# A decoder block's MLP: the second stage by seven block products instead of eight, with its operand sums made in the first stage

## The chip, the cores and the metric

The kernel runs on one core of a Trainium2 chip. The metric is the device time of one execution in microseconds (us), lower is better. All tensors are float32. The kernel that is changed is called before, the other one after. Line numbers (L923) are those of the kernel whose profile or listing is spoken of.

## The reference, cut to what matters

```python
# x: (1, 2048, 1024); D_MODEL = 1024; D_FF = 4096; one layer
h = _rmsnorm(x, norm_pre_mix)
...                                   # projections, attention, gated MLP, merge, w_out
x = x + _rmsnorm(y, norm_post_mix)

h = _rmsnorm(x, norm_pre_mlp)                                # 2048 x 1024
a = relu(einsum('bsd,df->bsf', h, w_mlp_in))                 # MLP, first stage: 2048 x 4096
y = einsum('bsf,fd->bsd', a * a, w_mlp_out)                  # MLP, second stage: 2048 x 1024
x = x + _rmsnorm(y, norm_post_mlp)
```

The change concerns the last four lines: two matrix products of 2048 x 1024 x 4096 each, a squared ReLU between them and a norm with a residual sum behind them.

## The kernel before, in words

Every float32 product is made of three reduced ones. `split` (L68) writes an operand as a rounded upper part, by an ACT copy at L71 or a POOL one at L73, and the rest, by a subtraction at L76. `mm3` (L85) then issues upper x upper, upper x rest and rest x upper (L86 to L88), all summed in one PSUM bank. `split_in` (L78) loads with a DMA on the SP queue (L82) and splits. So one block product 128 x 128 by 128 x 512 costs three matmuls on PE (TensorE). The order of the matmuls is the order in which the code issues them; the other engines' instructions are put in order by a scheduler, and each engine, the SP queue among them, runs its list strictly in that order.

The tokens are cut into two halves of 1024 (`half`; half 1 first), and each half into two blocks of 512. Ahead of the MLP, `out_block` (L754 and on) writes for each 128 tokens the sum `x` to `x1_d`, the normalized and transposed `h` to `h2_d`, and five sums of blocks of `h` (called T1 to T4 and B22) to `t_d` (L822). The sums of one half are gathered in the tile `tail` ahead of the last of these stores.

**The MLP's first stage** (about 1500 to 2147 us) already uses the scheme of Strassen and Winograd: a 2 x 2 by 2 x 2 block product by seven block products instead of eight. A pair `q` of two tiles of 128 of the 4096 (f) channels, with the depth 1024 cut in two, is one operand (A11 to A22 and the sums S1 to S4); two blocks of 512 tokens, cut along the depth as well, are the other one (B11, B21, B22 and the sums T1 to T4). `product(half, q, i)` issues product `i` of 12 matmuls (L918), so that the stage has 16 pairs x 2 halves x 7 x 12 = 2688 matmuls. `load_a` fetches the raw weights of a pair, 1 MB, into one of three buffers (L887); `sum_a` makes S1 to S4 of them on POOL (L899 to L902) and splits them. `places` gives the order: products 1 and 2 need only A11, A12, B11 and B21, so that at the beginning of a half those of `LEAD` = 5 pairs run ahead of the first product that needs a T; at its end those of `TRAIL` = 3 pairs do. `load_t` loads and splits a T block. The seven products are added as they come: ACT takes product 1 out of PSUM (`xs`), DVE adds products 6 and 7 to it (`u6`, `u7`, L937), and the four results are formed by L941 on DVE. ACT then applies the ReLU (L942; L933 for the first result), POOL squares (L922), and L923 stores the result with 2 KB rows to `s_d[f]`, four stores of 256 KB for a pair.

**The MLP's second stage** (2147.4 to 2846.0 us) is a plain product. It handles one half at a time, and in it groups of four f tiles. `load_w2` and `load_s` fetch and split a group's weights and squares one group ahead. `mlp_out` runs over eight blocks of 128 tokens and two width halves of 512 and issues 4 x 3 matmuls for each (L86 to L88); DVE copies (L1137) or adds (L1139) the bank to the running sum `acc`, of which there is one of 128 x 1024 for each of the eight token blocks. In a half's last group each block is ended at once: ACT squares with a row sum (L1142), POOL multiplies by the gain (L1143), DVE adds two row sums (L1145) and takes a root with ACT's help (`rstd_of`, L93 to L99), then multiplies and adds the residual from `x1_d` (L1150), and SP stores the result. The stage has 2 halves x 8 blocks x 2 x 32 tiles x 3 = 3072 matmuls.

## Time and profile before

| | |
|---|---|
| time, median of 3 runs | 2857.97 us (2854.01 to 2858.14) |
| time of the profiled execution | 2858.39 us |
| its span, from the first to the last record | 2856.3 us |
| granted TensorE clock, mean over the span | 0.989 |
| PE busy | 2787.4 us, 98% of the span, 13748 matmul records |
| DVE, ACT, POOL busy | 1464.7, 861.0, 760.5 us |
| DMA moved | 442.88 MB, mean 155 GB/s |

The profile is of one execution. An engine's busy time is the union of its instructions, without waits. A group row gives busy time and mean nanoseconds of one instruction, then the idle time ahead of them and what ended it, after an arrow. A window row gives its length, then for PE, PEld (weight loads, which overlap PE), DVE, ACT and POOL the busy time with the number of instructions, then the granted clock (1.00 is full), the DMA engines' busy share and GB/s. A row of a transfer group gives the number of transfers, KB of each and the median us from issue to landing. A row of the timeline gives the start, the length, the engine, and in square brackets the wait ahead and its releaser.

### The profile page before, as it was taken

The page shows a single profiled execution, that of the slowest core. Times are in us where ns is not written, and L with a number is a line of the kernel's source. Part 1 is how long each engine was busy: PE and PEld are TensorE (multiplying, and loading weights), DVE is VectorE, ACT ScalarE, POOL GpSimd, SP SyncE. Part 2 cuts the span into 40 slices and gives each one's busy share as a digit, 9 for nine tenths or more (in the row PEclk, how much of TensorE's full clock was granted, in tenths as well). Part 3 has the DMA queues.
Part 4 walks back from the last instruction along what each step waited for, and adds up shares of the span by engine and source line. Part 5 has one row for each costly group of instructions (what it writes and reads, how often), then busy time and mean ns, then how long its engine had stood idle before and what let it go on. Part 6 is the DMA issues. An engine that isn't in the chain of part 4 may idle for free.

```text
span 2856.3 us, 36699 instructions
## 1 busy us (share of the span) xinstructions
PE 2787.4 (98%) x13748; PEld 2347.7 (82%) x13748; DVE 1464.7 (51%) x2557; ACT 861.0 (30%) x1799; POOL 760.5 (27%) x591
## 2 busy tenths in 40 slices
PE   8999999999999999999998999999999999999998
PEld 8889888988878888777776888788878888888887
DVE  5654562434443353656556644654457444665445
ACT  5213111244443321443444433443332111211111
POOL 0340341200000023213026654555531001321012
PEclk9999999999999999999998999999999999999999
DMA  7544445465666563656467334633335223452232
GB/s 258 176 149 154 164 144 172 145 206 178 200 206 200 162 202 126 199 168 183 143 186 256 133 104 147 203 129 115 121 123 178 92 96 96 147 168 91 89 96 96
DMA packets 248849, 442.88 MB, mean 155 GB/s; under 512 B 18144, under 2 KB 106464, under 8 KB 248672
## 3 DMA queue, kind: packets, MB, share of 16 engines
q1 hardware_dynamic: 248672, 440.55, 47.8%
q8 instruction: 108, 1.77, 0.3%
q14 instruction: 69, 0.57, 0.1%
HBM read 299.77 MB, written 140.71 MB: 154 GB/s over the span
## 4 chain that ended last, share of the span: by engine, by line
PE 80%; DMA 6%; DVE 4%; POOL 4%; issue 4%; ACT 2%; SPq 0%; DVEq 0%; POOLq 0%; ACTq 0%
PE y L87 8%; PE y L86 8%; PE y L88 8%; PE ab L918 7%; PE ac L918 5%; PE aa L918 4%; PE g L88 4%; PE g L86 4%; PE g L87 4%; PE x L86 3%; PE x L87 3%; PE x L88 3%; PE pv L597 2%; DMA g<-gated 1%; PE pT L578 1%
## 5 line engine op out<-in xcount | busy, mean ns | idle before, releaser
L87 PE MATMUL y<-w,s 128*128 128x512 f32 x1024 | 399.6, 390 | 0.0
L86 PE MATMUL y<-w,s 128*128 128x512 f32 x1024 | 399.2, 390 | 0.0
L88 PE MATMUL y<-w,s 128*128 128x512 f32 x1024 | 398.3, 389 | 0.0
L71 ACT ACTIVATE s<-s 128x512 fp32r<-128x512 f32 x128 | 80.7, 632 | 494.1 <-DMA s<-sd 451.9
L1139 DVE TENSOR_TENSOR acc<-acc,y 128x512 f32<-128x512 f32 x240 | 159.2, 682 | 130.8 <-PE y L88 130.8
L86 PEld LDWEIGHTS y<-w,s 128*128 128x128 f32 x1024 | 192.2, 188 | 41.2
L88 PEld LDWEIGHTS y<-w,s 128*128 128x128 f32 x1024 | 192.2, 188 | 40.7
L87 PEld LDWEIGHTS y<-w,s 128*128 128x128 f32 x1024 | 192.3, 188 | 39.8
L73 POOL TENSOR_SCALAR w<-w2r 128x1024 fp32r<-128x1024 f32 x64 | 68.8, 1075 | 514.2 <-DVE acc L1139 253.8
L922 POOL TENSOR_TENSOR c<-c 128x512 f32<-128x512 f32 x128 | 151.4, 1184 | 201.4 <-ACT c L942 158.8
L918 PE MATMUL aa<-B,A 128*128 128x512 f32 x768 | 191.6, 402 | 8.4 <-ACT A L71 5.5
L918 PE MATMUL ab<-T,S 128*128 128x512 f32 x768 | 188.7, 394 | 9.8 <-ACT T L71 6.3
L918 PEld LDWEIGHTS aa<-B,A 128*128 128x128 f32 x768 | 147.6, 193 | 44.9 <-ACT A L71 6.8
L918 PEld LDWEIGHTS ab<-T,S 128*128 128x128 f32 x768 | 145.4, 190 | 42.9 <-ACT T L71 7.5
L86 PE MATMUL x<-hT_a,wq 128*128 128x512 f32 x384 | 149.7, 390 | 0.0
L88 PE MATMUL x<-hT_a,wq 128*128 128x512 f32 x384 | 149.4, 389 | 0.0
L87 PE MATMUL x<-hT_a,wq 128*128 128x512 f32 x384 | 149.4, 389 | 0.0
L73 POOL TENSOR_SCALAR w_g<-w_g_r 128x1024 fp32r<-128x1024 f32 x32 | 34.4, 1075 | 412.3 <-PE g L88 358.6
L76 DVE TENSOR_TENSOR w<-w2r,w 128x1024 fp32r<-128x1024 f32 x64 | 79.1, 1236 | 109.8 <-POOL w L73 109.8
L76 DVE TENSOR_TENSOR s<-s 128x512 fp32r<-128x512 f32 x128 | 93.5, 739 | 68.8 <-ACT s L71 68.1
L604 DVE TENSOR_REDUCE o<-po 128x256 f32<-128x512 f32 x48 | 33.2, 691 | 183.8 <-PE po L603 183.8
L71 ACT ACTIVATE S<-w1r 128x512 fp32r<-128x512 f32 x96 | 60.2, 631 | 154.9 <-PE ab L918 88.5
(276 smaller groups left out, 6546.5 us busy)
## 6 DMA issues: line engine op xcount, KB each, us to landing
sd<-c SPq DMA_DIRECT2D x128, 256.0 KB, 2.2
w1r<-in_w_mlp_in_dram SPq DMA_DIRECT2D x32, 1024.0 KB, 5.3
w2r<-in_w_mlp_out_dram SPq DMA_DIRECT2D x64, 512.0 KB, 3.6
s<-sd SPq DMA_DIRECT2D x128, 256.0 KB, 4.5
qk<-hl SPq DMA_DIRECT2D x24, 1024.0 KB, 5.3
qq<-qk SPq DMA_DIRECT2D x96, 256.0 KB, 5.0
w_g_r<-in_w_in_dram SPq DMA_DIRECT2D x32, 512.0 KB, 5.3
gated<-gt SPq DMA_DIRECT2D x64, 256.0 KB, 2.9
```

The costliest lines, as they stand in the source:

```text
L71: act.activation(hi, src, AF.Copy)
L73: pool.tensor_scalar(hi, src, 1.0, 1.0, op0=OP.mult, op1=OP.mult)
L76: (pool if lo_eng == "pool" else dve).tensor_sub(lo, src, f32(hi))
L86: pe.matmul(ps, lh, rh, start=start, stop=False)
L87: pe.matmul(ps, lh, rl, start=False, stop=False)
L88: pe.matmul(ps, ll, rh, start=False, stop=stop)
L578: pe.transpose(pt[:, off:off + P], e[:, b, hf * P:(hf + 1) * P], ident)
L597: pe.matmul(pv[:, o0:o0 + w_], l, r, start=n == 0, stop=n == len(mms) - 1, skip_group_check=True)
L604: dve.tensor_reduce(ot[:, :, j * 64:(j + 1) * 64], po.rearrange("p (b h e) -> p b e h", b=4, h=2), axis=AX.X, op=OP.add)
L918: pe.matmul(p, w[:, l, k, :], h[:, r, k, :], start=i in (1, 6, 5) and not k and not n, stop=k == 3 and n == 2, skip_group_check=True)
L922: pool.tensor_mul(t, t, t)
L1139: dve.tensor_add(an, an, p)
```

## The change: what it does

The second stage also becomes a 2 x 2 by 2 x 2 block scheme with seven products. Its blocks are: two blocks of 128 tokens, one from each 512-token block of a half (so a *token block* is one of eight pairs of these); two f tiles (a pair `q` of the first stage); two width halves of 512. One step (`ysteps`) is one group `g` of two pairs at one token block: seven products of 2 x 3 = 6 matmuls. There are 8 groups x 8 token blocks = 64 steps, and 64 x 42 = 2688 matmuls. The groups are the outer loop, so that the sums `acc` of all 2048 tokens stay on the chip (16 tiles of 4 KB per partition), and the weights are read once.

The operands of the left side, four squares and three sums, are made in the first stage: ACT now does ReLU and square (`square`), POOL makes four sums of squares for a pair (it did four squares), and `store_s` writes all seven to a new `s_d`, seven stores of 256 KB with 512-byte rows. The result tiles that are summed live longer, and SBUF is shared out anew: raw weights in five tiles of 512 KB instead of three of 1 MB, `c` tiles 3 instead of 6, `LEAD` 4 instead of 5. The T tiles of the first half are allocated up front in another order; `T2` no longer lies at the address of `tail`.

```diff
-    s_d = dtile([NF, P, S], "sd")
+    s_d = dtile([NF // 2, 2, P, 4, 7, P], "sd")
...
-    NQ, LEAD, TRAIL = NF // 2, 5, 3
+    NQ, LEAD, TRAIL = NF // 2, 4, 3
...
     def load_a(half, q):
-        raw = wp3.tile([P, 2, KT, P], F32, name=f"w1r_{half}{q}", tag="w1r", bufs=3)
-        sp.dma_start(raw.rearrange("p f k c -> p f (k c)"),
-                     a["w_mlp_in"][2 * q:2 * q + 2].rearrange("f p k c -> p f (k c)"))
-        araw[half, q] = raw
+        araw[half, q] = []
+        for f in range(2):
+            raw = wp3.tile([P, KT, P], F32, name=f"w1r_{half}{q}{f}", tag="w1r", bufs=5)
+            sp.dma_start(raw, a["w_mlp_in"][2 * q + f])
+            araw[half, q].append(raw)
...
-        def out_tile(f, ci, t):
-            pool.tensor_mul(t, t, t)
-            sp.dma_start(s_d[f, :, half * HALF + ci * 512:half * HALF + (ci + 1) * 512], t)
+        def store_s(o, t):
+            sp.dma_start(s_d[q, half][:, :, o, :], t.rearrange("p (i c) -> p i c", i=4))
+
+        def square(t, src):
+            act.activation(t, src, AF.Relu)
+            act.activation(t, t, AF.Square)
...
         elif i == 3:
-            output(0, 1, u_[half, q, 6], p)
+            a11, a12, a21, a22 = c1_[key], xs_[key], u_[half, q, 6], u_[half, q, 7]
+            output(a21, p)
+            s1, s2, s4 = (cp3.tile([P, 512], F32, name=f"s{n}_{nm}", tag="c", bufs=3) for n in (1, 2, 4))
+            pool.tensor_add(s1, a21, a22)
+            store_s(4, s1)
+            pool.tensor_sub(s2, s1, a11)
+            store_s(2, s2)
+            pool.tensor_sub(a21, a11, a21)
+            store_s(3, a21)
+            pool.tensor_sub(s4, a12, s2)
+            store_s(6, s4)
...
+    OPS = ("B11", "B21", "T2", "T3", "T1", "T4", "B22")
+    RIGHT, LEFT = 4, 14
+    def op_w2(q, name):
+        m = n_op[0] % (RIGHT + LEFT)
+        n_op[0] += 1
+        pl = r4 if m < RIGHT else bL
+        w = pl.tile([P, 2, 512], F32R, name=f"{name}y_{q}", tag="w2", bufs=RIGHT if m < RIGHT else LEFT)
+        raw = w2r_[q][:, dict(B11=0, B21=2, T2=4, T3=1, T1=0, T4=2, B22=3)[name]]
+        split(w[:, 0], w[:, 1], raw, "act", "pool")
+        w2_[q, name] = w
+    def load_s(n):
+        g, half, i = ysteps[n]
+        for q in (2 * g, 2 * g + 1):
+            pl = r4 if n % 3 == 0 else bL
+            w = pl.tile([P, 2, 7, P], F32R, name=f"s_{n}{q}", tag="s", bufs=2 if n % 3 == 0 else 4)
+            split_in(w, s_d[q, half][:, i], None, "act")
+            st_[n, q] = w
+    def yproduct(n, i):
...
+        which = {1: "a", 6: "a", 7: "a", 4: "a", 2: "b", 5: "c", 3: "c"}[i]
+        if i in (1, 2, 5):
+            ybank[n, which] = psum_any(f"y{which}_{n}")
...
+        if (half, b, ci, nh) in begun:
+            dve.tensor_add(an, an, p)
+        else:
+            begun.add((half, b, ci, nh))
+            dve.tensor_copy(an, p)
+        if g == NQ // 2 - 1:
+            left[n, ci] = left.get((n, ci), 4 if not ci else 3) - 1
+            if not left[n, ci]:
+                finish(half, b, ci)
+    yorder = sorted((7 * n + t, n, i) for n in range(len(ysteps))
+                    for i, t in ((1, 0), (2, 3), (6, 4), (7, 8), (5, 9), (4, 12), (3, 13)))
```

`yproduct` issues one product's six matmuls and then the DVE copy (L1207) or add (L1204) of its bank. `yorder` interleaves neighbouring steps: for PE the order is product 1 of step n, 7 and 5 of step n-1, 2 and 6 of step n, 4 and 3 of step n-1. Products 1, 6, 7 and 4 of a step use one bank after another, each adding on top. The loads of `s` go two steps ahead, into three sets of two buffers of 448 KB. `sum_w2` makes the sums of a pair's weights on POOL, and `op_w2` splits the seven operands with ACT and POOL during the group before. `finish` is the old end of a token block (squares, gain, root, residual), now for all sixteen blocks inside the last group's eight steps.

The following rows are the instructions in the order in which the built program has them, at three places. A row gives the line, the operation, output<-inputs and the shape; the digits behind a name tell its half and pair or its step.

The SP queue at the beginning of the MLP's first stage, before. `td_81` is the last store of T sums from `tail`, the `w1r` are raw weights by pair:

```order
L923 DMA sd_82<-c11_0_12938 128x512
L887 DMA w1r_10_13270<-in_w_mlp_in_dram 128x2x1024
L822 DMA td_81<-tail_12725 2560x1x128
L887 DMA w1r_11_13272<-in_w_mlp_in_dram 128x2x1024
L82 DMA T2_1_13263<-td_81 128x1024 x2
L82 DMA ar1_13_13310<-in_w_mlp_in_dram 128x512
L82 DMA T3_1_13329<-td_81 128x1024 x2
L887 DMA w1r_12_13336<-in_w_mlp_in_dram 128x2x1024
```

The same place after:

```order
L888 DMA w1r_100_13274<-in_w_mlp_in_dram 128x1024
L821 DMA td_81<-tail_12725 2560x1x128
L888 DMA w1r_101_13276<-in_w_mlp_in_dram 128x1024
L888 DMA w1r_110_13278<-in_w_mlp_in_dram 128x1024
L81 DMA T2_first_13267<-td_81 128x1024 x2
L888 DMA w1r_111_13280<-in_w_mlp_in_dram 128x1024
L888 DMA w1r_120_13282<-in_w_mlp_in_dram 128x1024
L888 DMA w1r_121_13284<-in_w_mlp_in_dram 128x1024
L81 DMA T3_first_13266<-td_81 128x1024 x2
```

The first pair's weights now come in two loads, the second of them behind the `td` store; three loads of 512 KB stand between `T2` and `T3`, and no lone `ar` load.

DVE at the start of the second stage, before. The c tiles are the last results of the first stage, `w2` and `s` are operands of the second one, `y` its banks:

```order
L941 TENSOR_TENSOR c11_015_17765<-u7_015_17750,ac_015_17752 128x512
L941 TENSOR_TENSOR c10_015_17782<-xs_015_17470,ab_015_17689 128x512
L941 TENSOR_TENSOR c01_015_17799<-u6_015_17702,ac_015_17752 128x512
L76 TENSOR_TENSOR w2_14_18013<-w2r_14_18014,w2_14_18013 128x1024
L1137 COPY acc10_17877<-y_1000_17885 128x512
L1137 COPY acc10_17877<-y_1001_17893 128x512
L1137 COPY acc11_17878<-y_1010_17901 128x512
L76 TENSOR_TENSOR s_120_17856<-s_120_17856 128x512
```

The same place after (`s_10` and `s_11` belong to step 1, `s_20` and `s_21` to step 2; `ya_0` is the first bank of step 0):

```order
L942 TENSOR_TENSOR u7_015_18023<-u7_015_18023,ac_015_18025 128x512
L942 TENSOR_TENSOR xs_015_17720<-xs_015_17720,ab_015_17954 128x512
L942 TENSOR_TENSOR u6_015_17967<-u6_015_17967,ac_015_18025 128x512
L75 TENSOR_TENSOR s_10_18162<-s_10_18162 128x896
L75 TENSOR_TENSOR s_11_18166<-s_11_18166 128x896
L75 TENSOR_TENSOR s_20_18174<-s_20_18174 128x896
L1207 COPY acc100_18189<-ya_0_18182 128x512
L1204 TENSOR_TENSOR acc100_18189<-acc100_18189,yb_0_18191 128x512
L75 TENSOR_TENSOR s_21_18178<-s_21_18178 128x896
L1207 COPY acc100_18189<-ya_0_18182 128x512
```

Three splits of `s` now stand ahead of the first copy, and a fourth between the second and the third reading of a bank.

DVE inside the second stage, before, where one group's adds and the next group's splits alternate:

```order
L1139 TENSOR_TENSOR acc16_17883<-acc16_17883,y_11260_18965 128x512
L1139 TENSOR_TENSOR acc16_17883<-acc16_17883,y_11261_18979 128x512
L1139 TENSOR_TENSOR acc17_17884<-acc17_17884,y_11270_18993 128x512
L76 TENSOR_TENSOR w2_120_19021<-w2r_120_19022,w2_120_19021 128x1024
L1139 TENSOR_TENSOR acc17_17884<-acc17_17884,y_11271_19007 128x512
L76 TENSOR_TENSOR s_1220_19052<-s_1220_19052 128x512
L76 TENSOR_TENSOR s_1221_19056<-s_1221_19056 128x512
L76 TENSOR_TENSOR s_1230_19065<-s_1230_19065 128x512
L1139 TENSOR_TENSOR acc10_17877<-acc10_17877,y_11600_19073 128x512
```

After, one step's worth of DVE (`ya_29` is the first bank of step 29, `yc_28` the third bank of step 28, `s_306` and `s_307` the operands of step 30):

```order
L1204 TENSOR_TENSOR acc010_18493<-acc010_18493,ya_29_20095 128x512
L1204 TENSOR_TENSOR acc001_18501<-acc001_18501,ya_28_20035 128x512
L75 TENSOR_TENSOR s_306_20027<-s_306_20027 128x896
L1204 TENSOR_TENSOR acc001_18501<-acc001_18501,yc_28_20110 128x512
L75 TENSOR_TENSOR s_307_20031<-s_307_20031 128x896
L1204 TENSOR_TENSOR acc010_18493<-acc010_18493,yb_29_20118 128x512
L1204 TENSOR_TENSOR acc010_18493<-acc010_18493,ya_29_20095 128x512
L1204 TENSOR_TENSOR acc001_18501<-acc001_18501,ya_28_20035 128x512
L1204 TENSOR_TENSOR acc000_18431<-acc000_18431,yc_28_20110 128x512
```

Two splits of 896 columns stand in every step between the adds, at fixed places of the cycle; the splits of `w2` are gone from DVE.

More of the change, by code (lines that the diff above doesn't have):

```diff
@@ L838, in block_kernel @@
     e3, er = ExitStack(), ExitStack()
-    s_, w2_, cnt, rls = {}, {}, [0], []
+    cnt = [0]
     def psum_any(name):
@@ L1153, in block_kernel @@
[L1153 to L1158 removed]
+    for j in range(2, 7):
+        ops_of(0, j)
+    load_s(1)
+    gfin = [rx.tile([P, 512], F32, name=f"gfin{n}", tag="c1", bufs=LEAD + 1) for n in range(2)]
+    for n in range(2):
+        sp.dma_start(gfin[n], bcast(a["norm_post_mlp"])[:, n * 512:(n + 1) * 512])
```

185 lines of the change are left out of this document (98 added, 87 removed).

## The prediction

> **What bounds the kernel now.** First I read the page's shares and the chain of work that ended last.
>
> ```profile
> span 2856.3 us, 36699 instructions
> PE 2787.4 (98%) x13748; PEld 2347.7 (82%) x13748; DVE 1464.7 (51%) x2557; ACT 861.0 (30%) x1799; POOL 760.5 (27%) x591
> PE 80%; DMA 6%; DVE 4%; POOL 4%; issue 4%; ACT 2%; SPq 0%; DVEq 0%; POOLq 0%; ACTq 0%
> ```
>
> PE (TensorE) is busy 98% of the span and carries 80% of the chain: the time is a count of matmuls times their spacing, plus the places where PE waits. Second, the windows, for the two stages that the change touches.
>
> ```profile
> 1600.00:1619.10 19.10, 19.10 (x86) 15.78 (x85) 12.26 (x15) 8.09 (x13) 14.47 (x12) 1.00 0.41 140
> 2147.40:2846.00 698.60, 698.60 (x3073) 576.56 (x3071) 375.95 (x559) 104.01 (x200) 106.67 (x91) 1.00 0.35 116
> 2802.30:2846.00 43.70, 43.70 (x193) 35.86 (x191) 30.43 (x63) 11.65 (x35) 17.82 (x14) 1.00 0.37 133
> ```
>
> The columns are length, then busy time of PE, PEld, DVE, ACT, POOL, granted clock, DMA share, GB/s. Row 2 is the whole second stage: PE never idle, clock 1.00, so 698.6 / 3072 = 0.2274 us per matmul. A first-stage product of 12 matmuls is 2.73 us and a pair of tiles (7 products) 19.1 us, which is row 1. Row 3 is the last group of the second stage: DVE is at 70% there, far above its 54% of the stage.
>
> **The change, part by part.** *Matmuls.* Second stage: 64 steps x 7 products x 6 matmuls = 2688 instead of 3072. The 384 fewer x 0.2274 = **-87.3 us**. The first stage keeps its 2688. A product is now 1.364 us, a step of seven 9.55 us.
>
> *Second stage, ordinary step.* Rows of the second stage before:
>
> ```profile
> L1139 DVE TENSOR_TENSOR acc<-acc,y 128x512 f32<-128x512 f32 x238 | 157.9, 682 | 130.8 <-PE y L88 130.8
> L76 DVE TENSOR_TENSOR s<-s 128x512 fp32r<-128x512 f32 x124 | 89.3, 728 | 68.8 <-ACT s L71 68.1
> L76 DVE TENSOR_TENSOR w<-w2r,w 128x1024 fp32r<-128x1024 f32 x60 | 73.4, 1224 | 106.3 <-POOL w L73 106.3
> L71 ACT ACTIVATE s<-s 128x512 fp32r<-128x512 f32 x124 | 78.3, 632 | 490.1 <-DMA s<-sd 447.9 <-PE y L88 39.8 <-DVE acc L1139 1.4
> L799 ACT ACTIVATE y<-xr x16: 1045/1060/1064, 1214.4 to 1508.8; 128x1024 f32<-128x1024 f32 x16
> ```
>
> The new split of 896 columns lies between 512 and 1024: 1.10 us on DVE, 0.95 on ACT. DVE per step: 7 adds x 0.682 + 2 x 1.10 = 7.0 of 9.55 us. ACT and POOL are far below. So PE stays the bound if the loads come in time. The loads form a loop: there are three sets of `s` buffers, so the load for step n+1 starts only when product 3 of step n-2 is done, which is the start of step n. Its first split stands on DVE ahead of the add that frees the bank of product 3 of step n-1. One turn is landing + 0.95 + 1.10 + 0.68 + product 1.36, less 0.68 (the first of the two tiles is free three matmuls early), plus some 0.3 for hand-overs (my estimate): landing + 3.7. It fits 9.55 us while the load lands within 5.8 us.
>
> ```profile
> sd<-c SPq DMA_DIRECT2D x128, 256.0 KB, 2.2
> w1r<-in_w_mlp_in_dram SPq DMA_DIRECT2D x32, 1024.0 KB, 5.3
> w2r<-in_w_mlp_out_dram SPq DMA_DIRECT2D x64, 512.0 KB, 3.6
> s<-sd SPq DMA_DIRECT2D x128, 256.0 KB, 4.5
> hT_b<-hTd SPq DMA_DIRECT2D x8, 512.0 KB, 7.2
> ```
>
> 512 to 1024 KB costs 1.7 us more, so 448 KB alone is about 3.4 us, the pair 4.9. The old `s` load waited in bunches behind `w2r`, hence 4.5; 7.2 is the worst row of this size. I take 3.4 and 4.9: no wait in most steps. Some three steps of eight also carry the 22 POOL operations of the next operands and 2 MB of `w2r`: between 0 and 10 us in all, taken as **+4**.
>
> ```profile
> L76 DVE TENSOR_TENSOR S<-w1r,S 128x512 fp32r<-128x512 f32 x96 | 86.2, 900 | 12.4 <-ACT S L71 11.1
> L941 DVE TENSOR_TENSOR c<-u,ac 128x512 f32<-128x512 f32 x64 | 43.8, 685 | 69.8 <-PE ac L918 53.9 <-POOL w1r L900 15.8
> ```
>
> These two rows have one shape in one stage; the split, whose inputs are both in SBUF, is 0.2 us dearer on average. The Trainium skill's "SBUF — State Buffer", section "SBUF: two separate sides", says that a VectorE operation with two SBUF inputs and a GpSimd operation that reads SBUF lock each other out for a whole instruction. By that rule each of the two splits could lose a POOL operation in those steps, which would be nearer the 10 than the 4; the averages here do not decide it.
>
> *Start of the second stage.* Count from the last first-stage matmul. Ten `w2` operand copies stand on ACT ahead of the splits of `s` for steps 1 and 2, because their first one needs the space of `B22`, read by that last matmul. 12 copies x 0.55 to 0.63 end at about 7; then three splits of 0.95 on ACT and 1.10 on DVE. On DVE all three stand ahead of the copy of product 1, which product 6 waits for: it is done at 11 to 12, and product 6 was due at 2.7. The fourth split's load stands on SP behind the last first-stage store, which waits for eight POOL operations of 1.3 to 1.5 (about 11.5); it lands at 15, is split at 17.4, and only then comes the copy that product 7 waits for: 18.1 instead of 5.5. Lost: 12.6, and about 1 for the clock (rows below): **+13.5**, between 5 (if the scheduler's order is kinder than this) and 18.
>
> *Last group.* The end of each token block now runs 16 times within 8 steps, beside loads.
>
> ```profile
> L1150 DVE SCALAR_TENSOR_TENSOR x<-acc,r_fin,x 128x1024 f32<-128x1024 f32 x6 | 7.7, 1285 | 0.6
> L99 DVE SCALAR_TENSOR_TENSOR t_fin<-r_fin,v_fin 128x1 f32<-128x1 f32 x7 | 4.7, 678 | 0.2
> L1145 DVE TENSOR_TENSOR fs<-fs 128x1 f32<-128x1 f32 x7 | 4.3, 612 | 6.0 <-ACT jk L1142 6.0
> L96 DVE RECIPROCAL r_fin<-r_fin 128x1 f32<-128x1 f32 x7 | 1.1, 164 | 1.2 <-ACT r_fin L93 1.2
> 2851.89 1.42 DVE L1150 SCALAR_TENSOR_TENSOR x<-acc,r_fin,x 128x512 f32<-128x512 f32 x2
> ```
>
> One end is 0.68 + 0.61 + four of about 0.16 + 1.42 (two halves, last row) = 3.3 us of DVE. A step with two ends is 7.0 + 6.7 = 13.7 us against 9.55 of PE. PE cannot run ahead: product 7 of a step waits for the add of product 6. Six such steps lose 4.1, one without loads 1.9, together 26.5, and DVE's waits for ACT's squares and roots some 3.5: **+30**; 13 if the small operations take their 0.16 throughout, 50 if two waits of each step lie bare.
>
> *First stage, inside.* Per pair POOL loses four squares and gains four sums; ACT gains four squares; SP issues 7 stores of 512-byte rows instead of 4 and two loads of 512 KB instead of one of 1024.
>
> ```profile
> L922 POOL TENSOR_TENSOR c<-c 128x512 f32<-128x512 f32 x128 | 151.4, 1184 | 201.4 <-ACT c L942 158.8 <-ACT c L933 37.5 <-DMA sd<-c 4.1
> L899 POOL TENSOR_TENSOR s<-w1r 128x512 f32<-128x512 f32 x32 | 41.8, 1307 | 66.4 <-DVE S L76 61.7 <-DMA w1r<-in_w_mlp_in_dram 4.7
> L900 POOL TENSOR_TENSOR w1r<-w1r 128x512 f32<-128x512 f32 x32 | 51.0, 1592 | 0.5
> L901 POOL TENSOR_TENSOR w1r<-s,w1r 128x512 f32<-128x512 f32 x32 | 47.9, 1496 | 2.3
> L902 POOL TENSOR_TENSOR w1r<-w1r 128x512 f32<-128x512 f32 x32 | 46.2, 1444 | 24.9 <-DVE A L76 23.4
> L942 ACT ACTIVATE c<-c 128x512 f32<-128x512 f32 x96 | 60.7, 633 | 48.7 <-DVE c L941 41.4
> td<-tail SPq DMA_DIRECT2D x4, 1280.0 KB, 6.3
> ```
>
> POOL: 10.6 becomes 2 x 5.84 = 11.7 of 19.1 us; ACT 7.5 becomes 10.0; traffic 2.75 MB per pair, 144 GB/s. The 512-byte rows moved 1280 KB in 6.3 us. PE's cover hides all of it: **0**, up to +10 if a store holds up the in-order SP queue; no gain, since PE is already never idle here.
>
> *The two beginnings of the first stage.* Two products (5.5 us) less are run ahead of `T2`, so PE asks for it earlier.
>
> ```profile
> 1521.19 0.52 SPq L822 DMA_DIRECT2D td<-tail  x1
> 1528.79 0.81 SPq L82 DMA_DIRECT2D T<-td  x2
> 1533.65 0.80 PE L918 MATMUL ab<-T,S 128*128 128x512 f32 x1 [5.56 <-ACT T L71]
> 1553.48 2.91 PE L918 MATMUL ab<-T,S 128*128 128x512 f32 x12
> 1532.00:1536.00 4.00, 1.43 (x3) 0.82 (x4) 2.79 (x2) 1.06 (x1) 3.84 (x3) 0.58 1.00 379
> 1804.00:1808.00 4.00, 2.13 (x10) 1.49 (x9) 3.13 (x4) 2.39 (x4) 1.56 (x1) 1.00 0.41 167
> 1844.57 16.74 PE L918 MATMUL aa<-B,A 128*128 128x512 f32 x60 [3.35 <-ACT A L71]
> ```
>
> `T2` no longer lies over `tail`, so its load need not wait for the last `td` store (issued 1521.2, 6.3 us, hence 1528.8). But half the first `w1r` is issued behind that store and three POOL sums follow, so the product starts near 1533.5 as before, with two products more still owed; `T3` then waits for a reused `w1r` buffer. I make it +4 (-3 to +10). The second beginning already waits 3.35 us at 1844; with two products less cover +2 (0 to +8). Together **+6**. The tail after the last matmul: two ends instead of one, **+2** (0 to 5).
>
> **Sum.** -87.3 + 4 + 13.5 + 30 + 0 + 6 + 2 = -31.8. The profiled execution took 2858.39 (span 2856.3 and 2.1 around it), 0.4 above the median 2857.97: 2826.6, called **2826**.
>
> **The rivals.** (1) *The load loop binds*, and it ends slower. At a landing of 7.2 (the `hT_b` row) a turn is 10.9 us, 1.35 too long in some 56 steps: +76, **2902**. It ends above the old time from a landing of 6.4 on (31.8 / 56 = 0.57 over 5.8). For it: reads of about this size took 6 to 7 us in crowded places. Against: the queue is only 35% busy here. (2) *The last group at half clock.* After the 5.56 us gap the granted clock fell to 0.58, and after a gap of 1.86 in the window from 1804 it stayed 1.00. If DVE's lag falls into one wait of 4 us per step, PE runs seven steps at 19.1 instead of 13.7: +38, **2865**. The Trainium skill's "TensorE: Matmul & The Clock Gate", Part 1, has the clock halve after one idle window of about 3.4 us; both rows agree with that. (3) *The last group stays covered*: the ends slip into DVE's gaps and the small operations are short: -30, **2797**. (4) The change does what it says as far as counts go; a smaller gain can only come from waits.
>
> **How the numbers follow.** Forecast 0.62, (1) 0.12, (2) 0.08, (3) 0.15, a wait not named 0.03. The range 2796 to 2866 takes in (2), (3) and the bounds of the start, the last group and the beginnings, and leaves out (1) with a little at either end. About 0.2% (5.7 us) is what a measurement of this kernel can tell from no change: faster 0.80, same 0.05 (mild forms of (1) and (2)), slower 0.15.
>
> **What would show it.** In the profile after: 2688 matmuls at 0.227 us in the second stage; PE idle about 12 us at its start, ended by DVE copies; no idle time in its middle (if ACT waits there for `s` and PE for DVE each step, it is (1)); PE at about 70% and DVE above 90% in the last 100 us with clock 1.00 (0.5 there is (2), PE full is (3)). The forecast is wrong if the middle loses more than 0.5 us per step, or if POOL or SP shows up as a releaser of PE in the first stage.

## The result, and the profile after

The changed kernel takes **2865.33 us** (median of 7, 2861.78 to 2870.05) against 2857.51 for the one before (median of 7): a ratio of 1.0035, 95% interval 1.0023 to 1.0046. It is slower by 0.35%, where 2826 and a gain of 1.1% were forecast.

The page's shares of after. The columns are those of the page shown for before:

```profile
span 2861.5 us, 36328 instructions
PE 2729.3 (95%) x13364; PEld 2287.1 (80%) x13364; DVE 1587.3 (55%) x2684; ACT 1039.1 (36%) x2039; POOL 1003.7 (35%) x703
```

PE has 384 matmuls less (13748 to 13364) and is busy 58 us less, but the span is 5.2 longer: what PE no longer works, it waits. Windows of after, by the starts of the stages' first matmuls. The rows are the first stage, the second stage, seven ordinary steps in its beginning, and its last group:

```profile
1502.20:2183.80 681.60, 632.62 (x2698) 515.40 (x2697) 355.22 (x418) 331.93 (x543) 404.35 (x272) 0.96 0.56 172
2183.80:2850.30 666.50, 631.94 (x2689) 508.67 (x2688) 490.24 (x687) 206.64 (x312) 293.47 (x199) 0.98 0.40 135
2214.10:2281.80 67.70, 67.70 (x295) 55.19 (x294) 48.54 (x63) 19.86 (x26) 27.57 (x19) 1.00 0.29 95
2742.40:2850.30 107.90, 91.36 (x361) 70.43 (x359) 96.04 (x187) 39.16 (x94) 48.10 (x36) 0.94 0.57 188
```

The same window of before for the first stage:

```profile
1502.00:2147.40 645.40, 625.42 (x2700) 510.25 (x2698) 348.24 (x424) 256.24 (x414) 348.70 (x268) 0.98 0.43 147
```

The second stage is 32.1 us shorter (698.6 to 666.5; forecast -39.8). The first stage has as many matmuls as before and is **36.2 longer** (forecast +6). That is where the gain went, and more.

Who made PE wait in the first stage, the waits of before and then of after (total, times, longest):

```profile
PE ab L918 <- ACT T L71: 6.3, 2, 5.6
PE aa L918 <- ACT A L71: 5.5, 3, 3.4
PE ab L918 <- DVE u L937: 3.6, 2, 1.9
```

```profile
PE ab L918 <- DVE u L939: 16.3, 5, 4.4
PE ab L918 <- ACT T_first L70: 15.9, 1, 15.9
PE aa L918 <- ACT A L70: 9.3, 2, 5.5
PE ab L918 <- DVE T_first L75: 5.2, 1, 5.2
```

The wait of 15.9 is the one for `T2` at the first beginning, which is mostly a matter of fewer products run ahead (it is 15.7 in before_lead4 below, which has that part of the change alone). Of the others, the waits for DVE's `u` have grown from 3.6 to 16.3 and those for ACT's `A` from 5.5 to 9.3. One for `A`, followed back through four engines at the second beginning. The timelines are of PE, ACT, SP and POOL of after:

```profile
1859.29 2.93 PE L918 MATMUL aa<-B,A 128*128 128x512 f32 x6 [3.81 <-ACT A L70]
```

```profile
1858.61 0.63 ACT L70 ACTIVATE A<-ar 128x512 fp32r<-128x512 f32 x1 [4.05 <-DMA ar<-in_w_mlp_in_dram]
```

```profile
1853.28 0.51 SPq L924 DMA_DIRECT2D sd<-u  x1
1854.98 0.51 SPq L924 DMA_DIRECT2D sd<-s  x1
1855.59 0.58 SPq L81 DMA_DIRECT2D ar<-in_w_mlp_in_dram  x1
```

```profile
1853.22 1.74 POOL L961 TENSOR_TENSOR s<-xs,s 128x512 f32<-128x512 f32 x1
```

PE waits for ACT's copy of a lone load `ar` (the weights of products 1 and 2 that run ahead). ACT waits for the load. SP issues it 0.6 us after a store of a sum, and SP issues that store at 1854.98, when POOL has just ended the sum (1853.22 + 1.74). So a load of weights, which depends on nothing that POOL does, stands behind POOL in SP's queue. How common this is shows in the group of POOL's first weight sum, before and then after:

```profile
L899 POOL TENSOR_TENSOR s<-w1r 128x512 f32<-128x512 f32 x32 | 41.8, 1307 | 66.4 <-DVE S L76 61.7 <-DMA w1r<-in_w_mlp_in_dram 4.7
```

```profile
L899 POOL TENSOR_TENSOR s<-w1r 128x512 f32<-128x512 f32 x32 | 43.8, 1369 | 191.6 <-DMA w1r<-in_w_mlp_in_dram 183.8 <-DVE S L75 7.8
```

It waited 4.7 us for raw weights in all, and now waits 183.8. Most of this PE does not feel: in the middle of the first half, matmuls 336 to 1092, it lost 1.3 us, against 0.9 before. At the beginnings and just behind them, where operands are made just in time, it does.

### The profile page after: what moved, and what is told of

Same layout as the page of the kernel before. It is cut to its first block, busy times and chain, and to the rows that moved or that the text cites. A ratio compares the mean times of both kernels' runs of the same rounds, so it can differ in the third digit from the quotient of the medians.

```text
span 2861.5 us, 36328 instructions
## 1 busy us (share of the span) xinstructions
PE 2729.3 (95%) x13364; PEld 2287.1 (80%) x13364; DVE 1587.3 (55%) x2684; ACT 1039.1 (36%) x2039; POOL 1003.7 (35%) x703
## 5 line engine op out<-in xcount | busy, mean ns | idle before, releaser
L70 ACT ACTIVATE s<-s 128x896 fp32r<-128x896 f32 x128 | 121.9, 953 | 269.8 <-PE ya L1197 137.8
L1204 DVE TENSOR_TENSOR acc<-acc,ya 128x512 f32<-128x512 f32 x224 | 151.4, 683 | 80.2 <-PE ya L1197 79.7
L75 DVE TENSOR_TENSOR s<-s 128x896 fp32r<-128x896 f32 x128 | 169.5, 1326 | 44.6 <-ACT s L70 44.4
L918 PE MATMUL ab<-T_first,S 128*128 128x512 f32 x384 | 96.7, 402 | 24.2 <-ACT T_first L70 15.9
L1197 PE MATMUL ya<-T2y,s 128*128 128x512 f32 x384 | 100.0, 396 | 13.8 <-ACT s L70 13.8
L1197 PE MATMUL ya<-B11y,s 128*128 128x512 f32 x384 | 103.0, 405 | 9.9 <-DVE acc L1204 9.9
L899 POOL TENSOR_TENSOR s<-w1r 128x512 f32<-128x512 f32 x32 | 43.8, 1369 | 191.6 <-DMA w1r<-in_w_mlp_in_dram 183.8
L1197 PE MATMUL yc<-B22y,s 128*128 128x512 f32 x384 | 100.8, 398 | 8.2 <-DVE acc L1204 8.2
L918 PEld LDWEIGHTS ab<-T_first,S 128*128 128x128 f32 x384 | 74.8, 196 | 41.5 <-ACT T_first L70 16.3
L85 PE MATMUL g<-hT_b,w_g 128*128 128x512 f32 x256 | 105.6, 412 | 0.0
L75 DVE TENSOR_TENSOR S<-w1r,S 128x512 fp32r<-128x512 f32 x96 | 95.5, 996 | 18.0 <-ACT S L70 17.0
```

The source lines that it names most:

```text
L70: act.activation(hi, src, AF.Copy)
L75: (pool if lo_eng == "pool" else dve).tensor_sub(lo, src, f32(hi))
L85: pe.matmul(ps, lh, rh, start=start, stop=False)
L899: pool.tensor_add(s1, a21, a22)
L918: pe.matmul(p, w[:, l, k, :], h[:, r, k, :], start=i in (1, 6, 5) and not k and not n, stop=k == 3 and n == 2, skip_group_check=True)
L1197: pe.matmul(p, s[:, l], w[:, r], start=i in (1, 2, 5) and not m and not o, stop=m == 1 and o == 2, skip_group_check=True)
```

## The experiments

Theories on the first stage: **Q**, loads stand behind stores of POOL's sums in SP's queue; **D**, there are fewer buffers ahead (`LEAD` 4, weights in five half tiles); **L**, POOL's sums keep POOL busy and hold up DVE's operations with two SBUF inputs; **C**, formed later, the lone loads wait for `c` tiles, of which three instead of six are left and which hold the sums until these are stored.

All lengths below are read like those above, from the first first-stage matmul to the first of the second stage and on to the end of the last one. They are compared rather than totals where they can be, since the part ahead of the first stage, which no run changes, took from 1500.1 to 1513.5 us in the profiled executions. "Lost" is the distance between the starts of two numbered first-stage matmuls, less 0.2267 us for each. The beginnings are matmuls 0 to 252 and 1092 to 1512, the first ordinary pairs behind them 252 to 336 and 1596 to 1680. Each row's lengths come from one profiled execution, up to 7 us away from the median beside it. Where runs have the same first stage it came out within 1.3 us (after and two runs further below: 681.7, 681.5, 682.8; own_act and one further below: 647.0, 645.9). The start of the second stage did not repeat so well, as is shown there.

| run | median us | ratio to before, 95% | first stage | second stage | lost: first beginning | second beginning | first ordinary pairs |
|---|---|---|---|---|---|---|---|
| before | | 1 | 645.4 | 698.6 | 21.6 | 10.4 | 0.0 |
| after | 2865.3 | 1.0023 to 1.0046 | 681.7 | 666.4 | 26.3 | 29.2 | 13.3 |
| sums_pool | 2863.7 | 1.0013 to 1.0037 | 667.6 | 680.6 | 25.8 | 20.7 | 7.0 |
| no_sums | 2818.4 | 0.9855 to 0.9885 | 639.2 | 663.0 | 27.3 | 0.4 | 0.1 |
| before_lead4 | 2866.7 | 1.0021 to 1.0047 | 651.4 | 698.6 | 27.6 | 10.2 | 0.1 |
| w1r_act | 2848.0 | 0.9963 to 0.9985 | 665.3 | 666.0 | 26.1 | 26.9 | 0.1 |
| sums_dve | 2846.8 | 0.9957 to 0.9976 | 659.3 | 666.2 | 25.8 | 10.0 | 6.9 |
| ar_act | 2850.5 | 0.9974 to 0.9993 | 659.2 | 670.7 | 25.8 | 21.0 | 0.2 |
| combo | 2847.1 | 0.9957 to 0.9980 | 666.9 | 670.8 | 26.3 | 14.3 | 8.8 |
| combo2 | 2844.8 | 0.9954 to 0.9980 | 654.7 | 665.6 | 23.3 | 10.6 | 4.1 |
| combo_mix | 2840.0 | 0.9940 to 0.9973 | 659.0 | 662.4 | 27.0 | 15.8 | 3.5 |
| ar_own | 2868.5 | 1.0029 to 1.0059 | 676.4 | 673.7 | 23.5 | 20.1 | 19.4 |
| own_act | 2842.9 | 0.9941 to 0.9969 | 647.0 | 672.1 | 20.4 | 15.1 | 0.1 |
| own_act_mix | 2841.2 | 0.9931 to 0.9966 | 650.2 | 662.9 | 21.9 | 10.1 | 3.3 |
| own_act_dve | 2856.1 | 0.9984 to 1.0006 | 660.3 | 665.0 | 24.4 | 9.4 | 11.9 |

### The first stage: queue, depth, or GpSimd

**sums_pool.**

```diff
-            sp.dma_start(s_d[q, half][:, :, o, :], t.rearrange("p (i c) -> p i c", i=4))
+            (pool if o in (2, 3, 4, 6) else sp).dma_start(s_d[q, half][:, :, o, :], t.rearrange("p (i c) -> p i c", i=4))
```

> The changed kernel, but the four stores of the sums that GpSimd makes in the first stage (L924, operands 2, 3, 4 and 6 of each pair) are issued from GpSimd's own queue instead of SP's. Theory Q (queue): SP runs in order, and a store that waits for a GpSimd sum holds back the loads of weights behind it. Then the first stage (681.7 us) loses 15 to 28 us, and the waits of TensorE near 1603, 1859, 1886 and 1944 us go; total 2838 to 2850. Theory D (depth): the loads are late because there are fewer buffers (five tiles of 512 KB, three c tiles, LEAD 4). Then the first stage stays within 5 us of 681.7, total 2861 to 2870. Theory L (GpSimd's load): GpSimd is late by its own work, and the issuing of four more stores makes it later: total 2865 to 2880.

The first stage lost 14.1 us less, for Q, but the second stage took 14.2 more, and the total is no better. The groups of sums_pool in its first stage (1560 to 2140) show the price of issuing on GpSimd, and what became of DVE's splits beside it (953 ns each in after):

```profile
L75 DVE TENSOR_TENSOR S<-w1r,S 128x512 fp32r<-128x512 f32 x87 | 133.1, 1530 | 0.8
...
L924 POOL DMA_DIRECT2D sd<-s x87 | 65.3, 751 | 23.4 <-POOL s L961 11.8 <-POOL s L955 11.3 <-DMA w1r<-in_w_mlp_in_dram 0.4
```

**no_sums.** The four `pool` sums are taken out; the stores name tiles that exist: `store_s(4, a21)`, `store_s(2, a11)`, `store_s(3, a21)`, `store_s(6, a12)`.

> The changed kernel without GpSimd's four sums of squares in the first stage: all seven stores stay, but the four of the sums store squares that are there already (so the second stage works on other numbers). Theory Q: no store waits for GpSimd any more, the first stage falls from 681.7 by 15 to 30 us, total 2835 to 2850. Theory L gives the same here, 15 to 30 us. Theory D: the loads still lack buffers, first stage within 6 us of 681.7, total 2860 to 2868.

42.5 us less in the first stage, and the second beginning loses next to nothing (0.4). So the sums are the cause of the whole loss. Which way they act (Q, L, or C) this run cannot tell, since with them go POOL's work, the late stores and the sums' `c` tiles.

**before_lead4.** In the kernel before, `LEAD` 4 with its order, and `load_a` of after with five half tiles.

> The kernel before, with the loading part of the change alone: LEAD 4 instead of 5 (with its order), and raw weights in five tiles of 512 KB instead of three of 1 MB; the second stage, the squares on GpSimd, the four stores and the six c tiles are those of before. Theory D: the first stage goes from 645.4 to 665 to 680 us, total 2877 to 2892. Theories Q and L: only the first beginning suffers (the second half of a pair's weights behind the td store, some 5 us), first stage 648 to 655, total 2861 to 2868.

The first beginning loses 6.0 more and nothing else changes: D is worth 6 us, as the prediction had it (+4), and not the 36.

**w1r_act**, and **ar_act** on top of it:

```diff
-            sp.dma_start(raw, a["w_mlp_in"][2 * q + f])
+            act.dma_start(raw, a["w_mlp_in"][2 * q + f])
...
-        split_in(w, a["w_mlp_in"][2 * q][:, n * 4:n * 4 + 4], raw, "act")
+        act.dma_start(raw, a["w_mlp_in"][2 * q][:, n * 4:n * 4 + 4])
+        split(w[:, 0], w[:, 1], raw, "act")
```

> The changed kernel, but the loads of raw weights in the first stage (L888) are issued from ACT's queue instead of SP's, where they stood behind the stores of GpSimd's sums; GpSimd's work is as before. Theory Q (queue): the weights come earlier, the first stage falls from 681.7 to 655 to 668 us, total 2838 to 2852. Theory L (GpSimd's sums make GpSimd late and lengthen DVE's operations with two SBUF inputs): the first stage stays between 676 and 688, total 2858 to 2870.

> As the run w1r_act, and the lone loads of raw weights at the beginnings and the end of a half (ar, L81 in lone_a) are issued from ACT's queue too; GpSimd's sums stay. In w1r_act the second beginning (matmuls 1092 to 1512 of the first stage) still lost 27 us, against 10 before the change and 10 with the sums on DVE. Theory Q (the rest of the loads still stands behind the stores of the sums): it falls to 8 to 14 us, total 2830 to 2838. Theory L (GpSimd's sums make its other work late and hold DVE's splits up): it stays at 20 to 28, total 2842 to 2850.

With POOL's work untouched, moving the loads off SP's queue gives 16.4 and then 22.5 us. The 13.3 lost at the first ordinary pairs are gone entirely, PE's waits for `u` fall from 16.3 to 4.6 us in w1r_act, and POOL's first weight sum in ar_act waits 40.4 us for raw weights instead of 183.8:

```profile
L900 POOL TENSOR_TENSOR s<-w1r 128x512 f32<-128x512 f32 x32 | 43.6, 1362 | 51.8 <-DMA w1r<-in_w_mlp_in_dram 40.4 <-DVE u L940 11.1
```

Together with sums_pool, which moved the stores instead of the loads, this shows Q. But ar_act's second beginning still lost 21.0, which is inside what L had foretold (20 to 28) and not the 8 to 14 of Q. And its total is no better than w1r_act's: the second stage gave back 4.7, at its start (further below). ACT's waits in ar_act between 1512 and 2172 name another cause:

```profile
ACT u L928 <- DMA ar<-in_w_mlp_in_dram: 12.5, 2, 6.5
...
ACT A L70 <- DMA sd<-s: 4.2, 2, 2.1
...
ACT u L928 <- DMA sd<-s: 3.9, 1, 3.9
```

An ACT copy does not itself use a sum. What fits is that ACT, which now issues the lone loads, waits to issue one into a `c` tile until the store of the sum that lies there has landed. This is theory C; the rows do not name the tile.

**sums_dve, combo, combo2, combo_mix** make the sums with other engines: all four by DVE with all loads on SP (sums_dve), with the raw weights on ACT's queue (combo), with the lone loads there too (combo2); combo_mix is combo with only the first two sums on DVE.

> The changed kernel with the four sums of squares of each pair made by DVE instead of GpSimd, stores on SP as in the change. Without any sums the first stage took 639.2 us. Theory L: GpSimd has half the work and DVE's splits are not held up; first stage 640 to 655, total 2822 to 2840. Theory Q says the same in kind, since DVE makes a sum in about half the time and the stores wait less: 645 to 665. If DVE becomes too full (four sums of about 0.68 us more for each pair of 19 us), the first stage stays above 670.

> The changed kernel with both: raw weights loaded from ACT's queue, and the four sums of squares made by DVE. If the two causes Q and L add up, the first stage falls from 681.7 to 643 to 652 us, total 2826 to 2836. If they are one and the same (each alone gave 16 and 22 us), it stays at 655 to 665, total 2838 to 2848.

> As combo, with the lone loads (ar) on ACT's queue too. Under Q the second beginning loses a few us less than in combo, first stage 640 to 650, total 2823 to 2834. If the ar loads wait for their c tiles rather than behind stores, they now hold ACT up, and it is 2 to 10 us slower than combo.

> As combo, but only the first two of the four sums (the ones that the others wait for) are made by DVE, the other two by GpSimd. If GpSimd's time for each pair is what counts (L), it lies between w1r_act and combo, first stage 650 to 660. If in combo DVE becomes the bound, this one is the faster: 640 to 650.

The sums on DVE give 22.4 us. With the raw weights on ACT's queue they give 14.8 (combo), less than either edit alone, and 27.0 with the lone loads there too (combo2). So the two do not add up. That does not make them one cause, since sums on DVE bring a loss of their own: the first ordinary pairs lost 8.8 in combo and 0.1 in w1r_act. All four versions are faster than the kernel before.

**ar_own, own_act, own_act_mix, own_act_dve.** The lone loads get two tiles of their own; two `c` tiles are left for the sums, one `s1`. ar_own has all loads on SP, own_act the weights on ACT's queue as in ar_act; own_act_mix and own_act_dve make the first two or all sums on DVE.

```diff
-            raw = cp3.tile([P, 512], F32, name=f"ar{n}_{half}{q}", tag="c", bufs=3)
+            raw = cp3.tile([P, 512], F32, name=f"ar{n}_{half}{q}", tag="ar", bufs=2)
```

> The changed kernel, but the lone loads (ar) have two tiles of their own; the sums are left with two c tiles instead of three, and the inner sum of load_a's weights with one instead of two (both can only make it slower). Loads stay on SP. Theory C (the lone loads wait for c tiles that hold GpSimd's sums until their stores have landed): the second beginning (matmuls 1092 to 1512) falls from 29 to 10 to 18 us, first stage 665 to 672, total 2846 to 2856. Theories Q and L: it stays at 25 to 33, first stage 678 to 690.

> As ar_act (raw weights and lone loads on ACT's queue, 659.2 us for the first stage) with the two tiles of their own for the lone loads. GpSimd's sums stay. Theory C with Q: the second beginning falls from 21 to 0 to 10 us, first stage 638 to 650, total 2822 to 2836. Theory L (GpSimd's own work): it stays at 18 to 24, first stage 655 to 664.

> As own_act, with the first two of the four sums on DVE. If the queue and the c tiles were all, it is within 5 us of own_act; if GpSimd's work still counts, it is 5 to 12 us faster.

> As own_act, with all four sums on DVE. If the queue and the c tiles were all, it is within 5 us of own_act or slower by DVE's load; if GpSimd's work still counts, it is 5 to 15 us faster.

own_act brings the first stage to 647.0, within 1.6 us of before, with all four sums still on GpSimd; the own tiles are worth 12.2 on top of ar_act. Of this, 5.9 lie at the second beginning, which still lost 15.1, more than the 0 to 10 expected (10.4 before the change). Another 5.4 lie at the first beginning (25.8 to 20.4), and no run shows that a lone load waits for a sum there. So the near equality with before is in part luck: the first beginning now loses 1.2 less than before's, the second 4.7 more.

ar_own alone gives 5.3, not the 10 to 17 that were expected. Its second beginning lost 20.1, 9.1 less than after's and between the two forecasts, but the first ordinary pairs lost 6.1 more: with the loads in SP's queue, free tiles help only in part.

Taking the sums off GpSimd now makes the first stage longer (+3.2 and +13.3). So L is not needed for the total. At the second beginning, though, it brings the loss to that of before (10.1 and 9.4), and what it costs appears elsewhere, 3.3 and 11.9 at the first ordinary pairs, where DVE now has the sums. So the queue (22.5) and the own tiles (12.2) together make up the 34.7 us. What the own tiles change at the first beginning is open, and so is whether the last 5 us of the second one are L or only sums that are ready later on GpSimd.

POOL's first weight sum in own_act waits for raw weights no longer. It still idles nearly as long, now for DVE's split of `S` (there is one `s1` tile here, two in after). So POOL's idle time by itself is not a measure of what PE loses:

```profile
L900 POOL TENSOR_TENSOR s<-w1r 128x512 f32<-128x512 f32 x32 | 48.5, 1517 | 173.5 <-DVE S L75 172.6 <-DMA w1r<-in_w_mlp_in_dram 0.9
```

Of the 34.7 us, 5.7 were given back at once in the second stage (666.4 to 672.1), by a longer wait at its start, the next subject.

### The start of the second stage

After, PE and then DVE at the start of the second stage:

```profile
2185.23 1.54 PE L1197 MATMUL yb<-B21y,s 128*128 128x512 f32 x6
2200.53 2.90 PE L1197 MATMUL ya<-T2y,s 128*128 128x512 f32 x6 [13.76 <-ACT s L70]
```

```profile
2184.05 0.69 DVE L942 TENSOR_TENSOR u<-u,ac 128x512 f32<-128x512 f32 x1 [2.03 <-PE ac L918]
2193.46 6.32 DVE L75 TENSOR_TENSOR s<-s 128x896 fp32r<-128x896 f32 x3 [8.73 <-ACT s L70]
2199.70 0.68 DVE L1207 COPY acc<-ya 128x512 f32<-128x512 f32 x1
```

Product 6 (`T2y`) starts when the copy of product 1 is done, and that stands behind the three splits, as foretold. (The bracket names an ACT copy that ended at the same time; the same wait in own_act is put to the DVE copy.) The splits took 2.1 us each, not 1.10: POOL was subtracting the `w2` operands beside them.

**start_dve** makes the first group's lower `w2` parts on DVE (`"dve" if q < 2 else "pool"` in `op_w2`).

> The changed kernel, with the lower parts of the first group's w2 operands subtracted by DVE instead of GpSimd (DVE was idle for 8.7 us there). Theory lock: at the start of the second stage the s splits on DVE take 1.1 instead of 2.1 us each, and the loads behind the last stores are issued earlier; the first two steps take 22 to 27 us instead of 30.3, total 2856 to 2862. Theory order, that of the prediction: ACT's ten copies and the three splits ahead of the first copy set the time; the first two steps stay at 28 to 32, total 2862 to 2868.

The first two steps took 28.4 us against 30.2 in after, within what the order theory gave, and the end of the first stage 5 more, where DVE now had this work as well. The three splits took 1.08 us each without POOL beside them. By the lock is meant that a DVE operation with two SBUF inputs and a POOL operation hold each other up. Measured against after's trace it is worth some 2 us.

But after's trace shows the kinder of two outcomes. In seven profiled executions (sums_pool, ar_act, ar_own, own_act, last_pool, no_gain, own_end) one split took 9.0 to 10.9 us. In last_pool and no_gain, described in the next section, nothing is edited at this place, and the first step took 24.6 us instead of 19.4. DVE and then POOL of no_gain there:

```profile
2195.66 11.24 DVE L75 TENSOR_TENSOR s<-s 128x896 fp32r<-128x896 f32 x3 [9.00 <-ACT s L70]
2206.83 0.68 DVE L1206 COPY acc<-ya 128x512 f32<-128x512 f32 x1
```

```profile
2195.36 1.26 POOL L961 TENSOR_TENSOR s<-xs,s 128x512 f32<-128x512 f32 x1
2196.58 2.50 POOL L75 TENSOR_TENSOR T1y<-w2r,T1y 128x512 fp32r<-128x512 f32 x2
2199.03 2.49 POOL L75 TENSOR_TENSOR T4y<-w2r,T4y 128x512 fp32r<-128x512 f32 x2
2201.47 2.50 POOL L75 TENSOR_TENSOR B22y<-w2r,B22y 128x512 fp32r<-128x512 f32 x2
```

POOL went through its row at 1.25 us each, and the first split took 9.24 of the 11.24 us and ended 0.9 after the row; in all seven it ended 0.9 to 1.0 us after POOL's row. In after both engines took 2.1 us for an operation while they worked side by side, by turns. So in the other outcome the lock sets the time: the copy of product 1 came 5 us later. What decides between the two is open. This is also most of what ar_act and own_act gave back in the second stage.

### The last group

Eight steps with two ends each took 107.9 us; 60 products (of 1.364 us) start in it, 81.9, so it lost 26.0 (1.1 of it by the wider spacing of all matmuls, below). **last_pool** gives the last group's lower `s` parts to GpSimd, **no_gain** leaves the line `pool.tensor_mul(y[:, nsl], y[:, nsl], gfin[n])` out, **own_end** is own_act with the end's small operations on GpSimd, own_end_mix adds two sums on DVE for the last two pairs of the first stage.

> The changed kernel, but in the last of the eight groups the lower parts of the s operands are subtracted by GpSimd instead of DVE (two of 896 columns a step). If DVE's work bounds the last group, as the prediction has it (13.7 us a step against 9.55), its 107.9 us fall by 14 to 22 us, total 2843 to 2852. If the waits of the chain of squares, sums and roots bound it, the group stays within 5 us of 107.9, total 2860 to 2868. If GpSimd, which also multiplies by the gain there, is too slow or holds DVE up, it takes longer: 2868 to 2885.

> The changed kernel without the multiplication by the last norm's gain, so GpSimd is idle in the last group of the second stage (the output lacks the gain). Theory lock: DVE operations with two SBUF inputs stand still while GpSimd works; in the last group DVE's 108.6 us hold 19.4 above the shortest of each kind. Then the last group falls from 107.9 to 86 to 94 us, total 2840 to 2850. Theory count, that of the prediction: DVE has 13.7 us of work a step whatever GpSimd does; the group stays between 103 and 109, total 2856 to 2867.

> As own_act (first stage 647.0 us), and in the ends of the last group the small operations on one value per token (sum of the two row sums, and four of the five steps behind the root) are done by GpSimd instead of DVE; the reciprocal, the adds and the residual stay on DVE. DVE's time in the last group held 25 us of these small operations, 12 of them waiting beside GpSimd. If DVE bounds the last group (the prediction's step, with the lock added), it falls from 107.3 to 86 to 95 us, total 2822 to 2834. If the chain of an end bounds it, GpSimd's slower steps make it 107 to 115, total 2842 to 2852.

> As own_end, and for the last two pairs of the second half the first two of the four sums are made by DVE, which is idle there. The start of the second stage took 26 us for its first step in own_act and 17 to 19 where the last sums were made earlier. If the last stores hold the first s loads back, the first step falls to 16 to 20 us and the total is 6 to 10 us under own_end's, 2814 to 2828; if not, it is within 3 us of own_end's.

| run | median us | ratio, 95% | first stage | first step of second | last group |
|---|---|---|---|---|---|
| after | 2865.3 | 1.0023 to 1.0046 | 681.7 | 19.4 | 107.9 |
| last_pool | 2871.9 | 1.0047 to 1.0083 | 681.5 | 24.6 | 110.8 |
| no_gain | 2855.7 | 0.9986 to 1.0005 | 682.8 | 24.6 | 96.1 |
| start_dve | 2869.2 | 1.0033 to 1.0064 | 686.7 | 18.1 | 107.6 |
| own_act | 2842.9 | 0.9941 to 0.9969 | 647.0 | 26.2 | 107.3 |
| own_end | 2852.7 | 0.9976 to 1.0001 | 645.9 | 26.3 | 117.7 |
| own_end_mix | 2852.7 | 0.9979 to 0.9997 | 652.7 | 16.6 | 116.7 |

Without the gain the group is 11.8 shorter. With the splits on GpSimd (last_pool) it is 2.9 longer, though DVE has two splits less in each step, so DVE's count alone is not the bound. DVE's groups in it, of after and then of no_gain:

```profile
L1182 DVE SCALAR_TENSOR_TENSOR acc<-acc,r_fin,x 128x512 f32<-128x512 f32 x28 | 23.7, 878 | 0.2
...
L1178 DVE TENSOR_TENSOR fs<-fs 128x1 f32<-128x1 f32 x15 | 7.6, 504 | 0.8 <-ACT jk L1176 0.8
L103 DVE TENSOR_TENSOR r_fin<-r_fin,t_fin 128x1 f32<-128x1 f32 x14 | 6.5, 466 | 0.0
...
L94 DVE TENSOR_SCALAR v_fin<-fs 128x1 f32<-128x1 f32 x14 | 2.1, 147 | 0.2
```

```profile
L1181 DVE SCALAR_TENSOR_TENSOR acc<-acc,r_fin,x 128x512 f32<-128x512 f32 x28 | 20.0, 746 | 0.1
...
L1177 DVE TENSOR_TENSOR fs<-fs 128x1 f32<-128x1 f32 x14 | 2.1, 153 | 1.3 <-ACT jk L1176 1.3
L103 DVE TENSOR_TENSOR r_fin<-r_fin,t_fin 128x1 f32<-128x1 f32 x14 | 2.1, 153 | 0.0
```

An operation on 128 x 1 with two inputs in SBUF took 504 and 466 ns on average beside POOL's gain, 153 without; with one such input (L94) it took 147 beside it. The averages hide two kinds: the median beside POOL was 0.16 us, the longest 1.25, about one POOL operation. So the lock costs DVE time. own_end takes small operations away from DVE as well, and the group gets longer. Its window, and whom DVE waits for in it (2720 to 2840):

```profile
2721.40:2839.10 117.70, 96.93 (x361) 73.23 (x359) 76.69 (x116) 38.68 (x90) 64.44 (x119) 0.89 0.52 171
```

```profile
DVE acc L1197 <- POOL r_fin L117: 19.4, 13, 3.9
```

DVE is busy 76.7 of 117.7 us, and PE still waits for its adds: the residual operation (L1197) waits for POOL's root steps, and the adds that free PE's banks stand behind it. Work taken off a full engine came back as a wait in its in-order list. What would bound the group with neither was not reached. own_end_mix moves a loss in the same way: the first step of the second stage took 9.7 less (4.0 because the first split began earlier, the rest because its splits took turns with POOL), but the end of the first stage 7.0 more. The best ratios were measured for own_act_mix (0.9948), own_act (0.9955) and combo_mix (0.9956), whose intervals overlap; each is faster than both kernels.

## Why the prediction was wrong, step by step

| term | forecast | measured (after less before) |
|---|---|---|
| 384 matmuls fewer | -87.3 | -87.3 |
| ordinary steps | +4 (0 to 10) | +13.8 |
| start of the second stage | +13.5 (5 to 18) | +16.4 |
| last group | +30 (13 to 50) | +24.9 |
| first stage, inside | 0 (0 to 10) | +13.3 |
| its two beginnings | +6 (-3 to +18) | +23.5 (4.7 and 18.8) |
| tail | +2 (0 to 5) | +1.0 |

With 0.2 ahead of the first stage and -0.5 elsewhere in it, the right column makes the 5.2 us of the spans. That 2865 still lies inside the range of 2796 to 2866 is luck: the top of the range was there for rival 2, a last group at half clock, which did not happen (0.94).

*The second stage* came out within 8 us, its mechanisms mostly as put. The load loop (rival 1) does not bind: PE is busy in the whole window of ordinary steps, clock 1.00, and the loads landed in time:

```profile
s<-sd SPq DMA_DIRECT2D x128, 448.0 KB, 3.8
```

The start was put together rightly but for the splits: 2.1 us each for 1.10. The prediction had the lock in view for ordinary steps and not here. And 16.4 is the figure of one trace; with the 24.6 of last_pool and no_gain it would be 21.6, outside the 5 to 18.

The ordinary steps cost more, for one thing that was not foreseen: where PE does not wait, its matmuls start 0.2304 us apart on average instead of 0.2274 (row 3 of the windows, 67.70 / 294, gives 0.2303), which is 8.2 us over 2688. It was 0.2304 to 0.2305 in every run of the changed second stage, whatever the other engines did. Steps without a wait took 9.64, 9.64 and 9.78 us in turn, a period of three, like the three sets of `s` buffers; the cause stays open. The other 5.6 are waits, most of them in the second step of groups 1 to 6, where the next operands are made (these six groups took 470.2 us, less 336 products of 1.364 and 6.1 of spacing). The last group's size was right, but its reason, a count of DVE's work, was half of it at most: 11.8 went with POOL's gain, beside which DVE's operations had lengthened. That the size came out is in part luck.

*The first stage* is the step that failed: "PE's cover hides all of it: **0**, up to +10 if a store holds up the in-order SP queue", and for the second beginning "with two products less cover +2 (0 to +8)". The mechanism was named and put in the wrong place. The prediction looked for its price in the middle, where PE has a pair's time of cover, and it was paid at the second beginning (18.8 where +2 was forecast) and at the first ordinary pairs behind both (13.3 where 0 was), where there is little. There the sums' stores, which wait for the last of four POOL operations in a row, stood ahead of the loads of weights (w1r_act, ar_act: 22.5). Of the 18.8, 8.2 went with the loads moved off the queue and 5.9 with the own tiles; the last 4.7 went only with sums taken off GpSimd. And one edit of the diff was not costed at all: `c` tiles 6 to 3, shared by lone loads and sums (own tiles are worth 12.2 in own_act, 5.9 of them at this place). The part that was costed, the shorter lead, was right: +4.7 measured at the first beginning, 6.0 alone in before_lead4. The sign that was to show the error, POOL or SP as a releaser of PE in the first stage, did not appear, since both acted through ACT and DVE: a sign has to be looked for along the whole chain, not in its last link. no_sums took 2818.4, close to the forecast, but is no proof of its other terms: its first stage was 6.2 us shorter than before's, where +6 was forecast, and its second stage began with 27.0 us for the first two steps instead of 30.2.

## What to carry to other kernels

When work is moved into a stage that "has room", don't ask whether its engines have time, but what stands behind each new instruction in an in-order queue: a store that waits for a slow engine holds up every load behind it, and this is paid where the pipeline is empty (at beginnings), not in the middle. Count every buffer that an edit takes away, and who shares it. Look at one place in several executions before giving it a price: here the same start took 19.4 us in one and 24.6 in two others. And taking work off a full engine helps only if the rest of its list does not then wait for the engine that got it.

## What the runs showed of the hardware

- Issuing a store from GpSimd's queue took GpSimd 0.75 us (sums_pool, 87 stores), and DVE's splits beside it went from 0.95 to 1.53 us. With weight loads issued from ACT's queue the same splits took 1.06 (w1r_act) and 1.05 us (ar_act).
- A DVE operation on 128 x 1 with two SBUF inputs took 0.15 us alone (no_gain), and 0.47 to 0.50 on average, 1.25 at most, beside GpSimd multiplications of 1.4 us (after).
- A DVE split of 128 x 896 took 1.08 us alone (start_dve) and 2.1 by turns with GpSimd subtractions, which also took 2.1 (after); in seven other executions one split took 9.0 to 10.9 us, until GpSimd's unbroken row of 1.25 us operations had ended (no_gain).
- The same matmul shape started every 0.2274 us in the second stage of before and every 0.2304 in that of after, at clock 1.00 in both.
